# One fixed expert fewer in the expert stage, and the shared expert's hidden pieces in blocks 2, 3 and 4

## The chip, the cores and the metric

The kernel runs on one core of a Trainium2 chip, in one launch. The metric is device time in microseconds (us) from the start to the end of an execution. The engines are called as in the profile: PE (TensorE, with PEld for its weight loads), DVE (VectorE), ACT (ScalarE), POOL (GpSimd) and SP (SyncE, which here only issues DMAs).

## What is computed

The reference applies two transformer-like blocks to 512 tokens of width 1024, in float32. The first has a gated delta rule with a convolution beside it, and then a mixture of experts; the second has a state-space mixer and a dense feed-forward layer. The change touches the mixture of experts alone, which the reference writes so (cut):

```python
scores = jax.nn.sigmoid((hf @ router_w).astype(jnp.float32))
...
_, top_idx = lax.top_k(jnp.where(exp_keep, sel, -jnp.inf), TOP_K)
...
def expert_block(args):
    tok, e = args
    return swiglu(h_pad[tok], w_gate[e], w_up[e], w_down[e])
...
routed = jnp.zeros((t + 1, d), h.dtype).at[slot_tok].add(weighted)[:t]
return (routed + swiglu(hf, s_gate, s_up, s_down)).reshape(bsz, n, d)
```

Each of the 512 tokens goes to 6 of 64 experts. Each expert is a gated feed-forward net with hidden width 256: gate and up matrices of 1024 x 256, a down matrix of 256 x 1024, 3 MB together. Every token also passes through one shared expert of the same size.

## The kernel before

**Blocks and ranks.** How many tokens an expert gets is known only on the chip, but the program's shape is fixed. So the kernel counts the tokens of the experts, sorts them by that count and gives the expert of each rank a place with a fixed number of rows (`CAPS`, by rank: 256, 192, 152, 128, ... 16). `plan` (from L1071) makes 42 blocks of up to 128 rows of it. The first 18 ranks (`NPAIR`) have an expert alone in a block (the largest three in two blocks), ranks 18 to 43 share a block two by two ("pair", 64 rows each), ranks 44 to 59 four by four ("quad", 32 rows each). Tokens beyond a rank's rows go to overflow blocks in a loop at the end; with the given inputs there are none, before or after the change.

The last four experts (`NFIX`) are left out of the sorting. They have fixed blocks 0 to 3 of 128 rows, and their weights are known without a count. So these blocks can run while DVE, ACT and POOL still build the tables of the ranked ones (`places`, `table`). The order before is: blocks 0 to 3 fixed, 4 quad, 5 and 6 rank 0, 7 and 8 rank 1, 9 quad, 10 and 11 rank 2, 12 quad, 13 rank 3, 14 quad, 15 rank 4, 16 pair, 17 rank 5, 18 pair, and from there a pair after each single rank, to block 41.

**One block** (`blocks` L1643, `ffn` L1597). POOL gathers the block's token rows from DRAM (`X<-hrow,tok`, L1593; `tokf` in place of `tok` in a fixed block). PE transposes them (`pt_xb`, 8 instructions, the copies L1341 and L1343 on ACT and DVE apply a scale and a shift), multiplies by the gate and up weights (`gub`, 16 instructions of 512 columns, 32 in a pair, 64 in a quad), ACT and DVE form the gated hidden (`sgb` L1615, `hb` L1617), PE transposes it (`pt_hb`) and multiplies by the down weights (`pyb`). POOL adds the rows to the result in DRAM (`yacc<-yb,tok`, L1639). The time of a matmul is set by its 512 columns and not by how many of the block's rows are filled. In a pair or quad the experts' matmuls run beside each other on parts of the array.

**Weights.** An expert is three loads of 1 MB on SP's queue: parts 0 and 1 for `gub`, part 2 for `pyb` (L1525; a ranked expert's number is read by a register load at L1511 ahead of them). A quad's order is four parts 0, four parts 1, four parts 2. Loads go in turn to a ring of 10 slots (`ew0` to `ew9`), from `more()` behind the tables on to 12 (two more, `ewx`, where the tables' one-hot rows were). A load waits until PE has read what the slot held 12 loads earlier; SP issues loads in order and keeps eight outstanding. The shared expert's three parts lie in slots of their own from early on.

**The shared expert's pieces.** Its hidden is made in four pieces of 16 matmuls (`shared`, L1540): `sg` of the first half ahead of block 0, and `su`, `sg`, `su` behind the blocks that `HID` names, 10, 11 and 12. Its output is four pieces of 8 matmuls (`spy`, `shared_out`, L1557) behind the blocks of `OUT`, 13 to 16. The hook of block 17 (`SECOND`) gives its three slots to the ring in place of the two `ewx`, and starts loads and DVE work for the second transformer block; until the slots are free SP waits there. A hook's code is written behind its block's `ffn`, so its matmuls stand behind that block's `pyb`. They need no weights from the ring.

**The order** on each engine is the order in which the instructions are written, but for what a scheduler moves by a few places, such as the `pt_xb` of the next block ahead of `pyb`.

In `body`, blocks 0 and 1 are written, then `table`, `more()`, and then

```python
            moe.blocks(bp, ps, {HID[0]: hid(0, 1), HID[1]: hid(1, 0), HID[2]: hid(1, 1), OUT[0]: out(0), OUT[1]: out(1), OUT[2]: out(2), OUT[3]: out(3), SECOND: second}, (2, len(BLOCKS)))
```

Of the kernel before, what the change touches and what calls it, by code (L numbers as in the profile page):

```python
# [826 lines left out]
def block_one(k, pool, early, two, route):  # L827
# [7 lines left out]
    with ExitStack() as es:  # L835
# [215 lines left out]


NE = 64
NFIX = 4
NRK = NE - NFIX
NPAIR, NQUAD = 18, 44
CAPS = [256, 192, 152, 128, 124, 118, 108, 100, 92, 88, 86, 82, 79, 76, 75, 72, 70, 68, 64, 64, 62, 62, 59, 57, 56, 54, 54, 52, 51,
        50, 49, 46, 45, 44, 44, 43, 42, 41, 41, 40, 39, 38, 37, 37, 32, 32, 32, 31, 30, 30, 28, 26, 25, 23, 22, 20, 20, 18, 17, 16]
CAPS = [-(-c // 16) * 16 for c in CAPS]
NOV = 72  # L1060
# [4 lines left out]
RINGX = 3  # L1065


HID, OUT, SECOND = (10, 11, 12), (13, 14, 15, 16), 17


def plan():  # L1071

    fixed = [(e, P, [("fix", NRK + e)]) for e in range(NFIX)]
    one, more, b, r = [], [], NFIX, 0
    while r < NRK:
        n = 1 if r < NPAIR else 2 if r < NQUAD else 4
        c = CAPS[r]
        if n == 1:
# [6 lines left out]
        else:  # L1085
            more.append([(b, P, [("rank", r + i) for i in range(n)])])
            assert max(CAPS[r:r + n]) <= P // n
            b += 1
# [22 lines left out]
NSLOT = NB * P  # L1111
STEP = [-(-c // P) * P if r < NPAIR else 64 if r < NQUAD else 32 for r, c in enumerate(CAPS)] + [P] * NFIX
CST2 = ["iota", "low", "col", "base", "cap"]


def const2():
# [6 lines left out]

        "base": np.broadcast_to(np.resize(np.concatenate([NFIX * P + np.cumsum([0] + STEP[:NRK - 1]), np.arange(NFIX) * P]), P)[:, None], (P, P)),
        "cap": np.broadcast_to(np.resize(np.array(CAPS + [P] * NFIX), P)[:, None], (P, P)),
    }
# [23 lines left out]
class Moe:  # L1150
# [426 lines left out]
    def parts(self, n):  # L1577
# [7 lines left out]
        t = {0: self.tok, 32: self.tok2, 64: self.tok3, 96: self.tok4}  # L1585
        return [(a, t[a][0:CAPS[r], b:b + 1]) for a, (_, r) in zip(range(0, P, m), whos)]

# [922 lines left out]
```

## Time and profile before

| | |
|---|---|
| time before, median of 3 runs | 2020.23 us (2017.06 to 2023.76) |
| the profiled execution, its own time | 2015.22 us |
| its span in the profile, mean granted clock | 2013.3 us, 0.968 |
| PE busy in the span | 1826.9 us (91%) |
| DVE, ACT, POOL busy | 993.3, 596.5, 502.1 us |
| expert weights: 192 loads of 1 MB in three names | `ewrank` x168, `ewx` x12, `ewfix` x12 |
| the first `gub` of block 0 | 587.61 us |
| the first `gub` of the first quad (block 4) | 645.67 us |

The chain that ended last runs mostly through PE, and is shared by many lines; in the expert stage `gub`, `pyb` and the loads of `ewrank` are its largest parts. The stage's blocks run from 587.61 us to about 1210 us. In it, read PE's busy time together with the share of the DMA engines: a window with a DMA share of 1.0 has all 16 DMA engines busy with weights and rows, a share below that has engines that stand still for part of it. The profiled execution is 5 us below the median of the three runs, and within 2 us of the lowest.

### The profile page before, as it was taken

How to read it: one execution, taken by the hardware profiler on the slowest of the kernel's cores; microseconds unless marked ns; L12 is line 12 of the kernel's file. 1: busy time of each engine (PE TensorE's matmuls, PEld its weight loads, DVE VectorE, ACT ScalarE, POOL GpSimd, SP SyncE). 2: the span in 40 equal slices, each digit the busy share in tenths (PEclk: the TensorE clock that was granted, in tenths of full speed). 3: DMA queues.
4: the chain of work that ended last, by engine and by line, in shares of the span. 5: the costliest groups of instructions: out<-in, count | busy, mean ns of one | idle time of the engine just before them, and what ended most of it. 6: DMA issues, size and time to landing. Idle time of an engine off the chain costs nothing.

```text
span 2013.3 us, 24229 instructions
## 1 busy us (share of the span) xinstructions
PE 1826.9 (91%) x8481; PEld 1237.6 (61%) x8481; DVE 993.3 (49%) x2220; ACT 596.5 (30%) x1124; POOL 502.1 (25%) x407
## 2 busy tenths in 40 slices
PE   5897778996879999989999987999999999999998
PEld 3686556885644333333333335888888788888886
DVE  4689955668776222262222227776423453323352
ACT  5453311213423111111111114433423344323341
POOL 1314343442422222212212225342001113101300
PEclk9998988998989999999999998999999999999999
DMA  8354353226488998999999983332323423233241
GB/s 313 118 179 161 88 163 99 80 60 214 151 299 300 355 369 346 350 398 380 367 366 370 375 321 127 111 106 79 115 89 92 143 85 105 89 94 100 79 141 42
DMA packets 135555, 393.64 MB, mean 196 GB/s; under 512 B 46899, under 2 KB 59443, under 8 KB 109064
## 3 DMA queue, kind: packets, MB, share of 16 engines
q1 hardware_dynamic: 109752, 363.66, 50.7%
q0 software_dynamic: 11856, 26.83, 5.3%
q10 hardware_dynamic: 13824, 1.58, 0.5%
q8 instruction: 68, 1.11, 0.2%
q14 instruction: 55, 0.45, 0.1%
HBM read 365.19 MB, written 38.54 MB: 201 GB/s over the span
## 4 chain that ended last, share of the span: by engine, by line
PE 69%; DVE 15%; DMA 10%; ACT 3%; issue 2%; POOL 1%; SPq 0%; another core or an unknown queue 0%; ACTq 0%; POOLq 0%; DVEq 0%
PE psi L139 12%; PE gub L139 10%; PE pof L139 9%; PE psf L139 9%; PE pyb L139 6%; DMA ewrank<-ew 6%; PE psco L139 2%; DVE cfa L746 2%; PE poo L139 2%; DVE gt L569 1%; PE pxca L139 1%; PE pt_xb L142 1%; PE pm L139 1%; PE psga L139 1%; PE psgb L139 1%
## 5 line engine op out<-in xcount | busy, mean ns | idle before, releaser
L139 PE MATMUL gub<-ewrank,xTb 128*64 128x512 f32 (+5 forms) x960 | 266.6, 596 | 1.2 <-DMA ewrank<-ew 0.6
L274 DVE TENSOR_TENSOR wlo<-wraw,whi 128x1024 fp32r<-128x1024 f32 (+1 forms) x103 | 121.7, 1182 | 137.7 <-ACT whi L273 136.9
L139 PEld LDWEIGHTS gub<-ewrank,xTb 128*64 128x64 f32 (+5 forms) x960 | 90.0, 141 | 158.3 <-issue 144.1
L273 ACT CAST whi<-wraw 128x1024 fp32r<-128x1024 f32 (+1 forms) x115 | 113.8, 989 | 226.5 <-PE psi L139 50.6
L139 PE MATMUL pyb<-ewrank,hTb 128*64 128x512 f32 (+5 forms) x440 | 152.4, 607 | 3.4 <-DMA ewrank<-ew 1.4
L139 PE MATMUL psi<-xnh,whi 128*128 128x512 f32 (+1 forms) x368 | 141.2, 385 | 0.0
L139 PE MATMUL psi<-xnl,whi 128*128 128x512 f32 (+1 forms) x368 | 140.9, 383 | 0.0
L1617 DVE SCALAR_TENSOR_TENSOR hb<-gub,tw,sgb 128x256 f32<-128x256 f32 (+5 forms) x38 | 18.3, 482 | 230.3 <-ACT sgb L1615 230.3
L1639 POOL DMA_INDIRECT yacc<-yb,tok x61 | 86.1, 1411 | 158.3 <-DVE yb L1631 109.3
L1341 ACT ACTIVATE xTb<-pt_xb,B,A 128x128 f32<-128x128 f32 (+5 forms) x168 | 74.0, 445 | 173.2 <-DVE xTb L1343 171.8
L139 PE MATMUL psi<-xnh,wlo 128*128 128x512 f32 (+1 forms) x296 | 112.8, 381 | 0.0
L1593 POOL DMA_INDIRECT X<-hrow,tok x38 | 39.6, 1042 | 291.2 <-PE pt_xb L142 285.9
L1343 DVE TENSOR_SCALAR xTb<-pt_xb,A,B 128x128 f32<-128x128 f32 (+5 forms) x168 | 65.5, 392 | 88.2 <-PE pt_xb L142 51.9
L2433 POOL TENSOR_TENSOR fr<-fr 128x512 f32<-128x512 f32 x32 | 48.6, 1518 | 238.2 <-ACT fr L2432 238.2
L139 PE MATMUL psf<-xml,whi 128*128 128x512 f32 (+1 forms) x272 | 102.6, 377 | 0.2 <-DVE xml L274 0.2
L139 PE MATMUL psf<-xmh,whi 128*128 128x512 f32 (+1 forms) x272 | 102.5, 378 | 0.2 <-ACT xmh L273 0.2
L139 PE MATMUL psf<-xmh,wlo 128*128 128x512 f32 (+1 forms) x272 | 102.5, 377 | 0.0
L1631 DVE TENSOR_TENSOR yb<-pyb,gt 128x512 f32<-128x512 f32 (+5 forms) x84 | 57.9, 690 | 72.0 <-PE pyb L139 70.5
L1615 ACT ACTIVATE sgb<-gub 128x256 f32<-128x256 f32 (+5 forms) x42 | 16.0, 382 | 260.3 <-PE gub L139 260.3
L139 PEld LDWEIGHTS pyb<-ewrank,hTb 128*64 128x64 f32 (+5 forms) x440 | 46.4, 142 | 74.9 <-issue 63.7
L139 PEld LDWEIGHTS psi<-xnh,whi 128*128 128x128 f32 x368 | 69.2, 189 | 13.8 <-issue 0.2
L139 PEld LDWEIGHTS psi<-xnl,whi 128*128 128x128 f32 x368 | 69.2, 188 | 13.4
(755 smaller groups left out, 4030.1 us busy)
## 6 DMA issues: line engine op xcount, KB each, us to landing
ewrank<-ew SPq DMA_DIRECT2D x168, 1024.0 KB, 25.1
wraw<-w_in SPq DMA_DIRECT2D x59, 512.0 KB, 3.7
wraw<-ff SPq DMA_DIRECT2D x32, 512.0 KB, 3.5
wf<-ff SPq DMA_DIRECT2D x64, 256.0 KB, 2.7
wm<-w_mod SPq DMA_DIRECT2D x28, 512.0 KB, 7.8
ewfix<-ew SPq DMA_DIRECT2D x12, 1024.0 KB, 16.9
ewx<-ew SPq DMA_DIRECT2D x12, 1024.0 KB, 19.6
wm<-w_mod SPq DMA_DIRECT2D x10, 1024.0 KB, 6.2
```

Source lines behind the costliest of these rows:

```text
L139: return self._done(self.eng.matmul(out, lhsT, rhs, **kw), rate, rhs)
L142: return self._done(self.eng.transpose(out, in_, ident), 0.00118, ident)
L273: nc.scalar.copy(hi, raw)
L274: (eng or nc.vector).tensor_tensor(lo, raw, hi.bitcast(F32), ALU.subtract)
L569: eng.tensor_tensor(t, S[0:nq, w:32, b:w].to_broadcast([nq, n, b]), S[0:nq, b:w, 0:b].to_broadcast([nq, n, b]), ALU.mult)
L746: V.scalar_tensor_tensor(a[:, r0 * 64:r1 * 64], y[:, (r0 + o) * 64:(r1 + o) * 64], w[:, j, 15 + o:16 + o], a[:, r0 * 64:r1 * 64], ALU.mult ...
L1341: nc.scalar.activation(dst(c), pt[:, i, :], AF.Identity, scale=sa, bias=sb)
L1343: nc.vector.tensor_scalar(dst(c), pt[:, i, :], sa, sb, ALU.mult, ALU.add)
L1593: self.k.nc.gpsimd.indirect_dma_start(out=X[0:idx.shape[0]], out_offset=None, in_=self.hrow, in_offset=bass.IndirectOffsetOnAxis(ap=idx, a ...
L1631: nc.vector.tensor_tensor(y[0:n, cs], py[0:n], self.gt2[0:n, cs], ALU.mult)
L1639: self.k.nc.gpsimd.indirect_dma_start(out=self.yacc[1 - self.nsc % 2], out_offset=bass.IndirectOffsetOnAxis(ap=idx, axis=0), in_=y[a:a + n ...
L2433: nc.gpsimd.tensor_tensor(r, r, r, ALU.mult)
```

## The change

`NFIX` goes from 4 to 3. Experts 61 to 63 keep fixed blocks, now 0 to 2. The expert that was the first fixed one joins the sorted ones, which are now 61 ranks: 19 alone, 26 in pairs, 16 in quads (`NPAIR, NQUAD = 19, 45`), with one more rank of 68 (80 after rounding up to 16) rows in `CAPS`. There are 42 blocks as before; one fixed block of 128 rows less, and one block of 80 rows more, near the end. All blocks in between move forward by one number: 0 to 2 fixed, 3 quad, 4 and 5 rank 0, 6 and 7 rank 1, 8 quad, 9 and 10 rank 2, 11 quad, 12 rank 3, 13 quad, 14 rank 4, 15 pair, 16 rank 5, 17 pair. `HID` goes from (10, 11, 12) to (2, 3, 4). `OUT` and `SECOND` keep their block numbers, and so lie one block later in the sequence.

```diff
-NFIX = 4
+NFIX = 3
 NRK = NE - NFIX
-NPAIR, NQUAD = 18, 44
-CAPS = [256, 192, 152, 128, 124, 118, 108, 100, 92, 88, 86, 82, 79, 76, 75, 72, 70, 68, 64, 64, 62, 62, 59, 57, 56, 54, 54, 52, 51,
+NPAIR, NQUAD = 19, 45
+CAPS = [256, 192, 152, 128, 124, 118, 108, 100, 92, 88, 86, 82, 79, 76, 75, 72, 70, 68, 68, 64, 64, 62, 62, 59, 57, 56, 54, 54, 52, 51,
...
-HID, OUT, SECOND = (10, 11, 12), (13, 14, 15, 16), 17
+HID, OUT, SECOND = (2, 3, 4), (13, 14, 15, 16), 17
```

The first place is PE's instructions behind `gub` of block 2. Before, from `pt_hb` of block 2 to `gub` of block 3, which is fixed (`ewfix`):

```order
L142 MATMUL pt_hb_5022<-cst,hb_5020 128x128 x2
L142 MATMUL pt_xb_5049<-cst,X_4567 128x128 x4
L139 MATMUL pyb_5028<-ewfix_2_4592,hTb_5025 128x512 x2
L139 MATMUL pyb_5032<-ewfix_2_4592,hTb_5025 128x512 x2
L142 MATMUL pt_xb_5058<-cst,X_4567 128x128 x4
L139 MATMUL gub_5067<-ewfix_0_5039,xTb_5048 128x512 x4
L139 MATMUL gub_5067<-ewfix_1_5041,xTb_5048 128x512 x4
```

After, from the same `pt_hb` to the start of `gub` of block 3, now the quad (`ewrank`), on PE:

```order
L142 MATMUL pt_hb_5017<-cst,hb_5015 128x128 x2
L139 MATMUL pyb_5023<-ewfix_2_4592,hTb_5020 128x512 x2
L139 MATMUL pyb_5027<-ewfix_2_4592,hTb_5020 128x512 x2
L139 MATMUL su_5031<-h_3610,ewshared_0_3915 128x512 x4
L139 MATMUL su_5031<-h_3610,ewshared_1_3917 128x512 x4
L142 MATMUL pt_xb_5111<-cst,X_4567 128x128 x4
L142 MATMUL pt_xb_5120<-cst,X_4567 128x128 x4
L139 MATMUL gub_5129<-ewrank_0_5085,xTb_5110 32x512
```

The piece `su` now stands between the last fixed block and the first quad, and all eight transposes of the quad's rows stand behind it, where four of them stood ahead of `pyb`.

The second place is PE's instructions in the two blocks of rank 2 and up to the quad behind them. Before, from `pyb` of rank 2's first block:

```order
L139 MATMUL pyb_5704<-ewx_4986,hTb_5701 128x512 x2
L139 MATMUL pyb_5708<-ewx_4986,hTb_5701 128x512 x2
L139 MATMUL su_5712<-h_3610,ewshared_0_3915 128x512 x4
L139 MATMUL su_5712<-h_3610,ewshared_1_3917 128x512 x4
L139 MATMUL gub_5757<-ewrank_0_5659,xTb_5738 32x512 x4
L139 MATMUL gub_5757<-ewx_4986,xTb_5738 32x512 x4
L142 MATMUL pt_hb_5770<-cst,hb_5768 128x32 x2
L142 MATMUL pt_xb_5864<-cst,X_4567 128x128 x3
L139 MATMUL pyb_5776<-ewx_4986,hTb_5773 32x512 x2
L139 MATMUL pyb_5780<-ewx_4986,hTb_5773 32x512 x2
L139 MATMUL sg_5784<-h_3610,ewshared_0_3915 128x512 x4
L139 MATMUL sg_5784<-h_3610,ewshared_1_3917 128x512 x4
```

After, the same two blocks on PE, from the same `pyb` to the start of the quad's `gub`:

```order
L139 MATMUL pyb_5676<-ewrank_2_5633,hTb_5673 128x512 x2
L139 MATMUL pyb_5680<-ewrank_2_5633,hTb_5673 128x512 x2
L139 MATMUL gub_5718<-ewrank_0_5629,xTb_5699 32x512 x4
L139 MATMUL gub_5718<-ewrank_1_5631,xTb_5699 32x512 x4
L142 MATMUL pt_hb_5731<-cst,hb_5729 128x32 x2
L142 MATMUL pt_xb_5814<-cst,X_4569 128x128 x3
L139 MATMUL pyb_5737<-ewrank_2_5633,hTb_5734 32x512 x2
L139 MATMUL pyb_5741<-ewrank_2_5633,hTb_5734 32x512 x2
L142 MATMUL pt_xb_5814<-cst,X_4569 128x128
L142 MATMUL pt_xb_5823<-cst,X_4569 128x128 x4
L139 MATMUL gub_5832<-ewrank_0_5788,xTb_5813 32x512
```

The two pieces between the blocks are gone, and so is the third behind the quad: from quad to quad PE now has only the work of the blocks.

## Rows read from the trace of the kernel before

**Rows 1.** the profile's page: shares of the chain by engine and line

```profile
PE psi L139 12%; PE gub L139 10%; PE pof L139 9%; PE psf L139 9%; PE pyb L139 6%; DMA ewrank<-ew 6%; PE psco L139 2%; DVE cfa L746 2%; PE poo L139 2%; DVE gt L569 1%; PE pxca L139 1%; PE pt_xb L142 1%; PE pm L139 1%; PE psga L139 1%; PE psgb L139 1%
```

**Rows 2.** windows: us; busy PE, PEld, DVE, ACT, POOL (instructions); clock; DMA share; GB/s

```profile
635.00:695.00 60.00, 53.26 (x229) 23.07 (x228) 23.81 (x112) 11.76 (x30) 14.52 (x12) 1.00 1.02 385
695.00:715.00 20.00, 19.02 (x82) 6.44 (x84) 5.41 (x11) 3.52 (x10) 4.77 (x4) 1.00 0.85 270
715.00:755.00 40.00, 36.79 (x151) 13.79 (x144) 8.08 (x17) 5.21 (x14) 9.06 (x7) 1.00 1.01 383
755.00:770.00 15.00, 14.93 (x84) 5.65 (x86) 2.46 (x6) 2.26 (x5) 2.38 (x2) 1.00 0.57 207
770.00:840.00 70.00, 65.37 (x280) 26.07 (x273) 18.50 (x35) 10.34 (x24) 17.94 (x14) 1.00 1.02 403
840.00:855.00 15.00, 13.86 (x60) 5.65 (x57) 4.13 (x8) 1.67 (x4) 2.80 (x3) 1.00 0.69 234
```

**Rows 3.** the chain in order of time: start us, us, what

```profile
672.53 6.88 PE gub L139 x16
...
685.48 6.88 PE gub L139 x16
...
711.13 7.12 PE gub L139 x64
...
720.25 3.64 PE pyb L139 x32
...
737.02 6.87 PE su L139 x16
...
756.17 7.06 PE sg L139 x16
...
796.70 3.43 PE spy L139 x8
...
809.69 1.92 PE pyb L139 x8
...
817.71 3.55 PE pyb L139 x20
821.26 7.08 PE gub L139 x16
```

**Rows 4.** the stage's start, in timelines of DVE, PE and POOL

```profile
572.96 2.50 DVE L1494 TENSOR_TENSOR onehots<-iota,fx_pl 128x512 fp32r<-128x512 f32 x4
...
631.59 7.03 PE L139 MATMUL gub<-ewfix,xTb 128*128 128x512 f32 x16
...
645.67 4.06 PE L139 MATMUL gub<-ewrank,xTb 128*32 128x512 f32 x35
...
625.63 1.11 POOL L1593 DMA_INDIRECT X<-hrow,tok  x1 [4.39 <-DVE tok L1464]
```

**Rows 5.** waits of SP's queue, 640 to 720 us (total, times, longest)

```profile
SPq L1525 <- PE gub L139: 33.2, 10, 16.0
```

**Rows 6.** DMA queues, 715 to 815 us: packets, MB, share of the 16 engines

```profile
q1 hardware_dynamic: 4528, 33.01, 80.4%
q0 software_dynamic: 1641, 3.62, 14.0%
```

**Rows 7.** windows of two late periods, columns as in group 2

```profile
951.60:979.50 27.90, 25.75 (x92) 9.54 (x92) 6.77 (x14) 5.00 (x12) 6.27 (x5) 1.00 1.00 367
1064.30:1093.50 29.20, 26.69 (x93) 9.30 (x93) 6.71 (x14) 4.92 (x12) 6.35 (x5) 1.00 1.01 375
```

**Rows 8.** waits of PE, 560 to 1260 us (total, times, longest)

```profile
PE pyb L139 <- DMA ewrank<-ew: 1.4, 3, 0.9
```

**Rows 9.** a window behind a long wait of PE, and the chain around it

```profile
880.00:900.00 20.00, 17.87 (x56) 7.86 (x57) 11.12 (x32) 3.79 (x9) 4.06 (x3) 0.88 1.02 407
...
846.88 3.70 PE pyb L139 x16
...
882.71 4.66 PE pyb L139 x16
```

## The prediction

> **What bounds the kernel now.** I read the page first: its table of engines has PE busy for 91% of the span, and the chain by line has `gub` and `pyb` of the experts beside one DMA, the expert weights [rows 1]. So PE's work counts nearly everywhere, and weights can count in the expert stage. There the windows decide [rows 2]. From 635 to 695, 715 to 755 and 770 to 840 us the DMA share is 1.01 or 1.02: the stream of weights and rows has no room. It stands still in part at three places: 695 to 715 (0.85 of 20 us, 3.0 us idle), 755 to 770 (0.57 of 15, 6.5 us) and 840 to 855 (0.69 of 15, 4.6 us). The chain shows what PE does at the second of these: one of the shared expert's pieces, `sg`, right behind another, `su` [rows 3]. Such a piece takes PE's time and frees no slot of the ring. Yet PE hardly waits for weights: `pyb` for `ewrank` 1.4 us in the whole stage [rows 8]. So the stage is balanced: the stream is full, PE is full, and the shared expert's pieces give the stream its time just where the three quads (blocks 9, 12, 14) want 12 loads each. The question is what happens when that cover is taken away.
>
> **The start.** One fixed expert fewer takes one of the four one-hot operations ahead of the first gather off DVE, 2.50 us for four [rows 4], so 0.6 us. The first ranked block's rows are asked for at 625.63 us [rows 4]. In the changed kernel PE wants them when `pyb` of block 2 and the piece `su` are done. `gub` of block 3 begins at 631.59 before, and the 6.87 us of `su` [rows 3] come in its place, so at 631.0 + 6.9 = 637.9 us. That leaves the gather 12 us. I cost it at nothing; `su` is the cover, and without it PE would wait for the rest of the gather. Start: **-0.6 us**.
>
> **The exchanged block.** From `gub` of block 3 to `gub` of the first quad are 645.67 - 631.59 = 14.1 us, which go [rows 4]. A single block has a period of 685.48 - 672.53 = 12.95 us [rows 3], which comes back near the end. Fewer rows don't shorten it: its matmuls keep their 512 columns. **-1.1 us**.
>
> **The moved pieces.** PE's work in them stays: three pieces of some 7.0 us (6.87 and 7.06 in [rows 3]), 21.0 together. What changes is what the weights do meanwhile.
>
> At blocks 2 to 4 the pieces hold PE for 21.0 us while the ring can't run ahead. A load needs the slot that PE has read, and SP's queue stood for 33.2 us behind `gub` in 640 to 720 us already [rows 5]; by 695 to 715 the stream idles for want of slots. The change puts more PE time there (21.0 less the 14.1 of the block that left) and takes three loads away. So the time is lost to the stream, and the ring is just as full, twelve loads, when the quad now numbered 8 comes. Its `gub` starts at 711.13 - 0.6 - 14.1 + 21.0 = 717.4 us.
>
> From there to `pyb` of the third quad (block 13 now) I hold PE's need against the stream's.
> - PE: before, 809.69 - 711.13 = 98.6 us [rows 3]. Without the three pieces and the output piece `spy` of 3.4 us, which lies behind block 13 afterwards, 74.1 us. Without a wait `pyb` would begin at 791.5.
> - Stream: 30 loads of 1.049 MB (12 + 3 + 12 + 3 of the next quad, rank and quad start from slots that the first quad frees). In 715 to 815 us the queue of SP carried 33.01 MB in 80.4 us of all engines' time, and the rows of tokens took 14.0 us [rows 6]. So 31.5 MB take 76.6 us, with the rows 90.6. The first slots come free with the half of a quad's `gub` (7.12 us), 3.6 us in: 721.0. The last weights land about 811.6.
>
> So PE waits 811.6 - 791.5 = **+20.1 us**, first in the quad that is block 11, then in block 13. Before, this stretch had a loss of its own: from 809.69 to 821.26 PE spent 11.6 us on `pyb` of the third quad and a `spy`, cut into pieces, where 3.64 and 3.43 are their durations elsewhere [rows 3]. With a few tenths between them that is some 4.1 us, which the new wait contains: **-4.1 us**.
>
> **Late in the stage.** A period of one single block and one pair takes 27.9 us early (951.60 to 979.50) and 29.2 late (1064.30 to 1093.50), with the DMA share at 1.00 and 1.01 [rows 7]. Five such late periods lose 6.5 us to the stream. Afterwards PE arrives later there: -0.6 - 1.1 + 20.1 - 4.1 = +14.3 us. The stream ends its third quad about when it did, and then has three loads more (7.7 us) and one block's rows (14.0 us for the six blocks 9 to 14, so some 2.3 us): at most +10. So it has more lead than before, and part of the 6.5 us comes back; the bounds are 0 and 6.5. I take **-4 us**, over half, since even the early period has a share of 1.00.
>
> **The clock.** Behind PE's long wait of before (6.5 us for `hb`) the granted clock was 0.88 over 20 us, so in part at the lower of the two levels, 1.2 GHz, and `pyb` of a pair took 4.66 instead of 3.70 us [rows 9]. Two long waits would cost 1 us each: **+2 us**, between 0 and 4. The Trainium skill (TensorE: Matmul & The Clock Gate, Part 1) says that an idle PE falls back to 1.2 GHz; the trace agrees with its 0.88.
>
> **Sum.** -0.6 - 1.1 + 20.1 - 4.1 - 4 + 2 = +12.3 us. On the profiled execution of 2015.2 us that gives 2027.5. This execution is near the fastest of the runs; their median is 2020.2, and on it the sum gives **2032.5 us**.
>
> **Rivals.**
>
> *Faster: the stream runs ahead.* If the ring is not full while the pieces run at blocks 2 to 4, the engines use these 21 us, quads 11 and 13 find their weights, and the wait of 20.1 us is gone with both losses of before: -0.6 - 1.1 - 4.1 - 6.5 = -12.3, 2007.9 us. It decides by the DMA's idle time between 640 and 718 us: each microsecond less takes one off the wait, and below 6 us of wait the kernel is faster by more than 0.3%. For it speaks that the share is 1.02 up to 695, so the ring is not full all the time. Against it: the twelve slots can't hold any load of block 11's quad but those behind the first quad's reads, whatever the lead [rows 5]. Chance 0.08.
>
> *No change to speak of: the stream is quicker in one long burst.* At the 403 GB/s of 770 to 840 us [rows 2] the 30 loads and their 3.4 MB of rows take 34.9 / 0.403 = 86.6 us, and the wait is 16 us. With all 6.5 us of the late loss regained and no loss by the clock: -0.6 - 1.1 + 16 - 4.1 - 6.5 = +3.7, 2024 us. Chance 0.20.
>
> *Heavier: nothing comes back.* At the 367 GB/s of the early period [rows 7] the same 34.9 MB take 95.1 us, the wait is 24.6 us, the late loss stays and the clock costs 2: +20.8, 2041 us. Chance 0.14. The Trainium skill (DMA: Bandwidth & Descriptors, Specifications) gives about 358 GB/s as HBM's limit for a core; by that the 34.9 MB would take an estimated 97.5 us and the wait would be 27 us. The trace has 403 GB/s over 70 us, so I don't hold to it.
>
> *It doesn't do what it says.* The order of PE's instructions has the pieces behind blocks 2, 3 and 4 and none between the later quads, so I give this nothing.
>
> **Chances and range.** A difference below 0.3% (6 us) can't be told from no change here. The forecast itself, from the +8 to +16 us that the bounds of its late and clock terms allow, has 0.58. Slower by over 0.3% are the forecast and the heavier case, 0.72. Within 0.3%: the second rival, 0.20. Faster: 0.08. The range reaches from below the second rival's 2024 to just above the heavier case's 2041, 2018 to 2042; what lies outside is the faster case (0.08) and the tails of the two others, some 0.1 together.
>
> **What would show it.** Right: the DMA share from 640 to 718 us well below the 1.02 of before, and near 1.0 from 720 to 811 without the gap at 755 to 770; PE's waits for `ewrank` at `gub` or `pyb` of blocks 11 and 13 near 20 us, where the stage had 2; late periods of 28 us and not 29.2; the granted clock below 1.00 around 770 to 810. Wrong: if PE waits for `X` of the first quad, the start was not covered; if `gub` of block 8 starts near 717 but no wait for weights follows, the ring held more than I think, and the first rival was right; if the late periods stay at 29.2, or grow, the stream and not PE ends the stage, and the time is that of the heavier case. The place is tested by `gub` of block 14: by the sum it starts near 811.6 + 3.6 + 3.4 = 819 us, against 821.26 before [rows 3], with one `spy` and one single block more to come.

## The result

The changed kernel takes 2031.2 us (median of 6 runs, 2028.69 to 2033.06) against 2019.38 us before (6 runs, 2017.06 to 2023.76): a ratio of 1.006, 95% interval 1.0048 to 1.0071. It is 12 us slower. The sum of the prediction had said +12.3 us, 2032.5 us, inside 2018 to 2042.

The profiled execution of the changed kernel took 2032.45 us, that of before 2015.22. So the two traces differ by 17.2 us where the medians differ by 11.8: before's execution is 4 us faster than its median, the other 1 us slower. Sizes of effects are therefore taken from medians here, and places and the lengths of single steps from traces.

The windows of the changed kernel at the borders of [rows 2], and from 680 to 851 us at borders that fit its own blocks (columns as there):

```profile
635.00:695.00 60.00, 54.79 (x225) 23.70 (x225) 21.11 (x96) 10.45 (x25) 12.64 (x10) 1.00 0.88 319
695.00:715.00 20.00, 18.02 (x54) 6.94 (x53) 4.39 (x10) 3.63 (x10) 2.52 (x2) 1.00 0.62 151
...
755.00:770.00 15.00, 13.34 (x89) 4.81 (x88) 3.38 (x8) 3.28 (x8) 2.41 (x2) 1.00 1.02 406
...
680.00:720.00 40.00, 36.95 (x127) 14.93 (x130) 10.15 (x22) 7.67 (x19) 7.31 (x7) 1.00 0.66 189
772.00:812.00 40.00, 29.51 (x119) 9.11 (x119) 5.86 (x12) 3.88 (x9) 8.98 (x7) 0.91 1.02 404
812.00:828.00 16.00, 15.57 (x52) 4.72 (x53) 4.31 (x8) 2.20 (x5) 1.05 (x1) 1.00 0.96 392
```

The DMA share is the eighth figure. It was 1.02 from 635 to 695 and 0.85 to 715; now it is 0.88 and 0.62, and from 680 to 720 only 0.66, with PE busy for 36.95 of 40 us. The gap at 755 to 770 is closed (0.57 before, 1.02 now). Behind it, at 772 to 812, the share is 1.02 and PE is busy for 29.51 of 40 us (37.52 before): where the kernel before had idle DMA time, this one has idle PE time, a hundred microseconds later.

SP's queue in 640 to 720 us shows why the stream stood still, as in [rows 5], where it was 33.2 us in all and 16.0 the longest:

```profile
SPq L1525 <- PE gub L139: 57.2, 6, 24.9
```

The loads wait for slots that PE has still to read, and the pieces behind blocks 2, 3 and 4 don't read any.

The second and the third quad (blocks 11 and 13) in PE's timeline (start us, us, line, operation, count, and in brackets the idle time before and what ended it):

```profile
766.38 2.56 PE L139 MATMUL pyb<-ewrank,hTb 128*32 128x512 f32 x8
...
769.56 1.90 PE L139 MATMUL pyb<-ewrank,hTb 128*32 128x512 f32 x4
...
772.03 3.62 PE L139 MATMUL pyb<-ewrank,hTb 128*32 128x512 f32 x20 [0.31 <-DMA ewrank<-ew]
775.58 3.70 PE L139 MATMUL gub<-ewrank,xTb 128*128 128x512 f32 x8
...
788.73 1.72 PE L139 MATMUL gub<-ewrank,xTb 128*32 128x512 f32 x6
792.50 4.41 PE L139 MATMUL gub<-ewrank,xTb 128*32 128x512 f32 x28 [2.04 <-DMA ewrank<-ew]
800.27 1.04 PE L139 MATMUL gub<-ewrank,xTb 128*32 128x512 f32 x2 [3.36 <-DMA ewrank<-ew]
803.67 1.91 PE L139 MATMUL gub<-ewrank,xTb 128*32 128x512 f32 x2 [2.35 <-DMA ewrank<-ew]
806.16 4.76 PE L139 MATMUL gub<-ewrank,xTb 128*32 128x512 f32 x26 [0.58 <-DMA ewrank<-ew]
811.98 0.44 PE L142 MATMUL pt_hb<-cst,hb 128*128 128x128 f32 x2 [1.05 <-DVE hb L1617]
```

From the first `gub` of the third quad to its `pt_hb` are 23.3 us. In the kernel before, the same step of its third quad took 8.2:

```profile
800.50 4.06 PE L139 MATMUL gub<-ewrank,xTb 128*32 128x512 f32 x35
...
808.74 0.44 PE L142 MATMUL pt_hb<-cst,hb 128*128 128x128 f32 x2 [1.16 <-DVE hb L1617]
```

Of the 15 us between them, PE's rows name 8.3 us of waits for `ewrank`; the rest stands in matmuls that the record shows as long (13.8 us of busy time for 64 that take 7.1 elsewhere). The list of waits, 788 to 812 us, has most of that rest in the row of the weight loads, PEld:

```profile
PEld gub L139 <- DMA ewrank<-ew: 13.3, 5, 4.3
```

Whoever goes by PE's row alone finds little more than half. Some 1.2 us more are the clock's: from 804 to 808 us the granted clock is 0.50, the lower level, and behind the last wait PEld goes from one group of four loads to the next in 0.86 us until 808.6, and in 0.43 from then on (busy time and the idle time ahead of it):

```profile
804.00:808.00 4.00, 3.42 (x14) 0.53 (x16) 0.00 (x0) 0.00 (x0) 0.00 (x0) 0.50 1.01 426
...
807.01 0.20 PEld L139 LDWEIGHTS gub<-ewrank,xTb 128*32 128x32 f32 x4 [0.66 <-issue]
...
809.04 0.12 PEld L139 LDWEIGHTS gub<-ewrank,xTb 128*32 128x32 f32 x4 [0.31 <-issue]
```

Behind it come the third quad's `pyb`, with the first output piece among them:

```profile
812.93 1.90 PE L139 MATMUL pyb<-ewrank,hTb 128*32 128x512 f32 x4
814.76 1.13 PE L139 MATMUL spy<-ewshared,shh 128*128 128x512 f32 x2
815.82 1.90 PE L139 MATMUL pyb<-ewrank,hTb 128*32 128x512 f32 x4
...
819.56 1.13 PE L139 MATMUL spy<-ewshared,shh 128*128 128x512 f32 x2 [0.35 <-DVE h L1568]
820.62 1.90 PE L139 MATMUL pyb<-ewx,hTb 128*32 128x512 f32 x4
...
827.06 7.13 PE L139 MATMUL gub<-ewrank,xTb 128*128 128x512 f32 x16
```

The next `gub` starts at 827.06, 14.1 us after the first `pyb`; 3.64 and 3.43 would be due [rows 3]. Before, the same step, also with one output piece in it, took 11.5 us (809.69 to 821.19 in PE's timeline, 821.26 in the chain of [rows 3]). No weight is waited for in these rows. The four `pyb` of one expert are written in a row and use the same quarter of the array, so they take 1.90 us by themselves, where 32 of four experts side by side take 3.64.

Late in the stage, two periods of one single block and one pair:

```profile
1042.70:1070.50 27.80, 25.61 (x93) 9.18 (x93) 6.71 (x14) 4.92 (x12) 6.30 (x5) 1.00 1.00 374
1070.50:1098.20 27.70, 25.55 (x92) 9.10 (x92) 6.71 (x14) 4.92 (x12) 6.35 (x5) 1.00 1.01 375
```

They last 27.7 to 27.8 us, as the early period of before (27.9) and not as its late one (29.2) [rows 7].

### The profile page after: what moved, and what is told of

Read it like the earlier page. It is cut to its first block, busy times and chain, and to the rows that moved or that the text cites. A ratio compares the mean times of both kernels' runs of the same rounds, so it can differ in the third digit from the quotient of the medians.

```text
span 2030.6 us, 24226 instructions
## 1 busy us (share of the span) xinstructions
PE 1834.3 (90%) x8477; PEld 1235.5 (61%) x8477; DVE 993.4 (49%) x2219; ACT 595.7 (29%) x1124; POOL 502.3 (25%) x407
## 4 chain that ended last, share of the span: by engine, by line
PE 71%; DVE 16%; DMA 6%; ACT 3%; issue 2%; POOL 1%; SPq 0%; another core or an unknown queue 0%; ACTq 0%; POOLq 0%; DVEq 0%
PE gub L139 12%; PE psi L139 12%; PE pof L139 9%; PE psf L139 9%; PE pyb L139 8%; PE psco L139 2%; DVE cfa L746 2%; PE poo L139 2%; DMA ewrank<-ew 1%; DVE gt L569 1%; PE pt_xb L142 1%; PE pxca L139 1%; PE pm L139 1%; PE psga L139 1%; DVE soq L462 1%
## 5 line engine op out<-in xcount | busy, mean ns | idle before, releaser
L139 PE MATMUL gub<-ewrank,xTb 128*64 128x512 f32 (+5 forms) x976 | 276.6, 601 | 10.7 <-DMA ewrank<-ew 8.3
L139 PE MATMUL pyb<-ewrank,hTb 128*64 128x512 f32 (+5 forms) x464 | 163.8, 607 | 2.8 <-ACT hTb L1622 0.8
L139 PEld LDWEIGHTS psi<-xnh,whi 128*128 128x128 f32 x368 | 69.6, 190 | 13.9 <-issue 0.2
```

What stands on the lines that cost most here:

```text
L139: return self._done(self.eng.matmul(out, lhsT, rhs, **kw), rate, rhs)
```

## The experiments

Theory A: the pieces' place is what costs, through the weight stream, which stands still for want of slots while they run. Rival B: the exchanged expert costs. Theory C, formed on the trace above: part of the loss is the order inside the third quad. All runs are compared with the kernel before on the same chip; ratios have 95% intervals.

**The two parts of the change, apart.** The first run keeps three fixed experts and puts the pieces back where they stood in the sequence:

```diff
-HID, OUT, SECOND = (2, 3, 4), (13, 14, 15, 16), 17
+HID, OUT, SECOND = (9, 10, 11), (13, 14, 15, 16), 17
```

> The changed kernel with the three hidden pieces back at the places of the sequence where they were before (blocks 9, 10 and 11 in the new count); three fixed experts stay. Theory A (the pieces' new place starves the weight stream: it idles at 680 to 720 us for want of slots, and PE then waits in the third quad): the idle stretch and the wait are gone, DMA share of 680 to 720 us back to 0.9 or more, under 3 us of waits for ewrank at gub and pyb, and the time falls by 10 to 14 us to 2017 to 2022 us. Rival B (it is the exchanged expert that costs, a late single block for a fixed one): the time stays at 2028 to 2033 us.

Measured: 2016.43 us (11 runs), ratio 0.9986 (0.9977 to 0.9995), 3 us below the kernel before and 15 below the changed one. The second has four fixed experts and moves the pieces alone:

```diff
-HID, OUT, SECOND = (10, 11, 12), (13, 14, 15, 16), 17
+HID, OUT, SECOND = (3, 4, 5), (13, 14, 15, 16), 17
```

> The kernel before with its four fixed experts, and only the pieces moved, to blocks 3, 4 and 5, which are the last fixed block, the first quad and the first block of rank 0, as in the changed kernel. Theory A (the pieces' place alone): 2030 to 2036 us, with the DMA share at 0.6 to 0.8 around 690 to 725 us and some 8 us of waits for ewrank at gub of block 14, the third quad. Rival B (the exchanged expert): no change, 2016 to 2023 us.

Measured: 2038.73 us (5 runs), ratio 1.0097 (1.0082 to 1.0112), 20 us slower, more than expected. Windows of the first run, then of the second, from 680 us on:

```profile
680.00:720.00 40.00, 36.79 (x178) 13.77 (x177) 9.91 (x21) 7.21 (x18) 8.78 (x7) 1.00 0.91 314
772.00:812.00 40.00, 37.42 (x160) 14.05 (x159) 9.63 (x19) 6.08 (x14) 7.58 (x7) 1.00 1.02 404
```

```profile
680.00:720.00 40.00, 36.85 (x107) 16.97 (x106) 9.25 (x20) 7.19 (x18) 7.45 (x7) 1.00 0.77 253
812.00:851.00 39.00, 30.93 (x107) 8.71 (x100) 4.80 (x9) 2.59 (x6) 3.73 (x3) 0.87 0.98 391
```

With the pieces back the stream's idle share is gone and PE is busy for 37.42 of 40 us at the third quad, which waits for no weight. With the pieces moved both signs are there, and the third quad, later in this kernel, has PE busy for 30.93 of 39 us. So the pieces' place costs, as A had it, and B falls: the run with the exchanged expert alone (with its output pieces one block later in the sequence) is 3 us faster, and the pieces cost 15 (three fixed) to 20 us (four). Whether the loss comes about as A says is left to the runs with short pieces.

**Why 15 and not 20.** With the pieces back, the first quad of the changed order has no `su` ahead of it. The row of its `pt_hb` in that run:

```profile
642.49 0.51 PE L142 MATMUL pt_hb<-cst,hb 128*128 128x128 f32 x2 [2.48 <-DVE hb L1617]
```

PE waits 2.48 us for `hb` where 1.1 is usual, and the granted clock is 0.59 from 642 to 646 us: the whole step from `pt_hb` of block 2 to that of block 4 is 30.9 us there (626.82 to 657.76), and in the changed kernel 42.4 (624.39 to 666.74) with 13.9 us of pieces in it, so 28.4 without. The piece behind block 2 hides some 2.5 us. With four fixed experts nothing is hidden: the step is 26.7 us before (640.70 to 667.44), and with the pieces 41.7 (642.80 to 684.53), so 27.8 without them.

Another part is the order inside the third quad. From its first `pyb` to the next `gub` the run with the pieces back takes 14.1 us, as the changed kernel does. The run with the pieces alone takes 14.1 as well, where the kernel before, with its output pieces behind the same blocks, took 11.5:

```profile
796.57 1.90 PE L139 MATMUL pyb<-ewrank,hTb 128*32 128x512 f32 x4
...
810.70 7.13 PE L139 MATMUL gub<-ewrank,xTb 128*128 128x512 f32 x16
```

```profile
831.58 1.90 PE L139 MATMUL pyb<-ewx,hTb 128*32 128x512 f32 x4
...
845.71 7.13 PE L139 MATMUL gub<-ewrank,xTb 128*128 128x512 f32 x16
```

So with four fixed experts the move of the pieces also changes how the third quad is written, which costs 2.6 us, and with three it does not. The whole sum, stretch by stretch, is in the table further down.

**What a piece costs where it stands.** Both kernels with the three pieces cut to an eighth:

```diff
-        for i in range(8):
+        m = 1 if up or f else 8
+        for i in range(m):
...
-                             start=(i == 0), stop=(i == 7))
+                             start=(i == 0), stop=(i == m - 1))
```

> The changed kernel with each of the three moved pieces cut to one of its eight matmul steps, behind blocks 2, 3 and 4; seven eighths of the shared hidden are left out, some 18.4 us of PE work. Theory A (there the pieces hold up the weight stream): the idle share of 680 to 720 us and the wait in the third quad shrink, and the time falls by 10 to 16 us, to 2015 to 2021 us, and comes within 4 us of the next run. Rival E (PE's work alone sets the time, wherever it stands): this run and the next each fall by 18 us, to 2013 and 1998 us.

Measured: 2018.17 us (10 runs), ratio 1.000 (0.9987 to 1.0013), 13 us less than the changed kernel.

> As the run with the pieces back at blocks 9, 10 and 11 (2016.4 us), with the same three pieces cut to one of eight steps there. Theory A (at 9 to 11 the stream of weights needs that time anyway, and PE would wait for weights in place of it): the time falls by 5 us at most, 2011 to 2017 us, and 10 us or more of waits for weights appear in the second and third quad. Rival E: it falls by the 18 us that are left out, to 1998 us.

Measured: 2015.4 us (10 runs), ratio 0.9988 (0.9978 to 0.9997), 1.0 us less than with the whole pieces by the medians, and nothing by the ratios (0.9986 there). So 18.4 us of PE work were worth 13 us behind blocks 2 to 4 and 1 us at most behind 9 to 11. Rival E, by which PE's work counts wherever it stands, falls. In the latter run 7.5 us of waits for `ewrank` are named at `gub` in PE's row and 13.8 in PEld's, where there were none with the whole pieces.

One expectation of theory A failed. With the pieces cut short at 2 to 4 the stream stands still less (share 0.86 at 680 to 720 us, not 0.66), but the wait in the third quad does not shrink: 8.1 us are named, 8.3 in the changed kernel:

```profile
680.00:720.00 40.00, 36.78 (x177) 13.65 (x176) 10.09 (x22) 7.68 (x19) 8.43 (x7) 1.00 0.86 288
...
PE gub L139 <- DMA ewrank<-ew: 8.1, 4, 3.4
```

The rows of `pt_hb` show what happens. The changed kernel, its blocks 0, 8 (the first ring-bound quad) and 13 (the third), the last one above at 811.98:

```profile
595.10 0.44 PE L142 MATMUL pt_hb<-cst,hb 128*128 128x128 f32 x2 [1.80 <-DVE hb L1617]
...
725.47 0.44 PE L142 MATMUL pt_hb<-cst,hb 128*128 128x128 f32 x2 [1.16 <-DVE hb L1617]
```

The run with the whole pieces behind 9 to 11:

```profile
597.53 0.44 PE L142 MATMUL pt_hb<-cst,hb 128*128 128x128 f32 x2 [0.99 <-DVE hb L1617]
...
709.61 0.44 PE L142 MATMUL pt_hb<-cst,hb 128*128 128x128 f32 x2 [1.16 <-DVE hb L1617]
...
795.62 0.44 PE L142 MATMUL pt_hb<-cst,hb 128*128 128x128 f32 x2 [1.08 <-DVE hb L1617]
```

With an eighth of them there, blocks 8 and 13:

```profile
709.01 0.44 PE L142 MATMUL pt_hb<-cst,hb 128*128 128x128 f32 x2 [1.16 <-DVE hb L1618]
...
795.98 0.44 PE L142 MATMUL pt_hb<-cst,hb 128*128 128x128 f32 x2 [1.05 <-DVE hb L1618]
```

With an eighth of them behind 2 to 4, blocks 0, 8 and 13:

```profile
598.12 0.44 PE L142 MATMUL pt_hb<-cst,hb 128*128 128x128 f32 x2 [2.00 <-DVE hb L1618]
...
712.45 0.44 PE L142 MATMUL pt_hb<-cst,hb 128*128 128x128 f32 x2 [1.16 <-DVE hb L1618]
...
798.34 0.44 PE L142 MATMUL pt_hb<-cst,hb 128*128 128x128 f32 x2 [1.05 <-DVE hb L1618]
```

Six kernels by such rows, in us; with four fixed experts the blocks are 9, 14 and 15 in place of 8, 13 and 14:

| kernel | `pt_hb` of block 0 to 8 | 8 to 13 | 13 to 14 | 14 to the last block |
|---|---|---|---|---|
| before (four fixed) | 121.9 | 89.5 | 20.6 | 377.1 |
| pieces alone (four fixed) | 143.7 | 87.4 | 23.2 | 378.3 |
| pieces back (three fixed) | 112.1 | 86.0 | 23.2 | 387.0 |
| changed (three fixed) | 130.4 | 86.5 | 23.2 | 386.9 |
| short pieces at 2 to 4 | 114.3 | 85.9 | 23.2 | 386.2 |
| short pieces at 9 to 11 | 112.5 | 87.0 | 23.2 | 386.8 |

With three fixed experts the move adds 18.3 us ahead of block 8 (21 less the 2.5 that are hidden), and the stretch from 8 to 13 doesn't get shorter by the 21 us of pieces that left it: 18.3 + 0.5 + 0 - 0.1 us in the four columns. With four fixed experts they are 21.8 - 2.1 + 2.6 + 1.2, 5 us more. In this stretch there are two limits of nearly the same length, as its windows in the two runs with pieces at 9 to 11 show, whole and short:

```profile
709.61:795.62 86.01, 80.51 (x363) 31.77 (x363) 18.06 (x37) 12.65 (x31) 20.34 (x16) 1.00 0.94 370
```

```profile
709.01:795.98 86.97, 74.00 (x321) 24.94 (x321) 18.07 (x37) 12.65 (x31) 20.37 (x16) 0.94 1.02 403
```

With the whole pieces the stream has room (0.94) and PE waits for no weight: the 86.0 us are PE's own, 65.0 of blocks (before: 89.5 less 24.4 of pieces) and 21.0 of pieces. With short ones, or none, PE waits for weights and the share is 1.02. So the stream's standing still at 680 to 720 us is not what makes the wait. The wait is there with and without work in front; what the move does is to put 21 us of PE's work where nearly all of it counts, and to take it out of a stretch that the weights make as long without it.

**The order inside the third quad.** The changed kernel with its output pieces one block later:

```diff
-HID, OUT, SECOND = (2, 3, 4), (13, 14, 15, 16), 17
+HID, OUT, SECOND = (2, 3, 4), (14, 15, 16, 17), 18
```

> The changed kernel with the output pieces one block later (behind 14 to 17, the second block's preparation behind 18), so that no spy stands inside the third quad's pyb. Theory C (the 14.2 us from the first pyb of the third quad to the next gub come from the order on PE: its pyb are written expert by expert between pieces of spy, so that they don't run beside each other; 7 us are lost to it, not to weights): the stretch without spy takes some 6 us, and the time falls by 4 to 7 us to 2024 to 2027 us. Rival D (PE is there as late as the weights let it be, and the order is hidden behind the stream): the time stays within 2 us of 2031.

Measured: 2025.17 us (5 runs), ratio 1.0034 (1.002 to 1.0047), 6 us less than the changed kernel, as C had it. From the first `pyb` of its third quad to the next `gub` are 8.0 us (811.04 to 819.03). But two numbers moved. The preparation of the second transformer block alone, behind 18:

```diff
-HID, OUT, SECOND = (2, 3, 4), (13, 14, 15, 16), 17
+HID, OUT, SECOND = (2, 3, 4), (13, 14, 15, 16), 18
```

> The changed kernel with the preparation of the second transformer block behind block 18 in place of 17, and nothing else. Theory F (of the 6 us that the run with the outputs moved had gained, about half came from this: SP's wait there falls from 21.9 us, and DVE's work of it lies elsewhere): 2025 to 2029 us, with SP's wait at that place under 15 us. Rival C (all of it came from the third quad's pyb being written without pieces of spy between): within 2 us of 2031.

Measured: 2033.21 us (5 runs), ratio 1.008 (1.0067 to 1.0094): no gain, though SP's wait there fell from 21.9 to 14.6 us as F wanted, so F falls. And the first output piece alone, out of the third quad, one block earlier:

```diff
-HID, OUT, SECOND = (2, 3, 4), (13, 14, 15, 16), 17
+HID, OUT, SECOND = (2, 3, 4), (12, 14, 15, 16), 17
```

> The changed kernel with its first output piece behind block 12, ahead of the third quad, in place of behind 13, the others behind 14 to 16, and the second block's preparation behind 17 as it was. The third quad's pyb has no spy inside, as in the run with the outputs moved, but that run's other edit (preparation behind 18) is not in it. Theory C (the order inside the third quad): the piece stands where PE waits for weights anyway, so it is free (3.4 us), and the quad's pyb take 3 us less: 2024 to 2027 us. Rival G (the run with the outputs moved gained by having the last output piece in the stretch of the preparation, not by the quad): 2029 to 2033 us.

Measured: 2028.56 us (6 runs, 2025.92 to 2032.61), ratio 1.0053 (1.0034 to 1.0071), between what C and its rival expected. Its third quad:

```profile
811.92 1.90 PE L139 MATMUL pyb<-ewrank,hTb 128*32 128x512 f32 x4
...
814.01 1.90 PE L139 MATMUL pyb<-ewrank,hTb 128*32 128x512 f32 x4
...
819.91 7.13 PE L139 MATMUL gub<-ewrank,xTb 128*128 128x512 f32 x16
```

Eight microseconds from the first `pyb` to the next `gub` in place of 14.1, of which 3.4 are the piece that left; two experts are still written by themselves. In this one trace `pt_hb` of block 14 comes at 828.04 and not 835.19, 6.6 us less counted from `pt_hb` of block 0 (594.51 and 595.10); the medians show 2.6 us, and the intervals of the two ratios overlap. By the rows 3.4 of the 6.1 us are the piece, which PE now does where it would wait for weights, and 2.7 are the order. So that the order costs time is shown by the rows; its price in the whole time isn't. The run with the outputs moved has the same 2.7 us. Its other 3.4 are the piece, too: from block 14 to the last block it takes 386.3 us with one output piece more than the changed kernel has there in 386.9. So its gain comes about half from the order, as C has it, and half from a piece that costs nothing where it stands now, which is nearer to rival G.

**Together.**

```diff
-HID, OUT, SECOND = (2, 3, 4), (13, 14, 15, 16), 17
+HID, OUT, SECOND = (9, 10, 11), (14, 15, 16, 17), 18
```

> Pieces back at blocks 9, 10 and 11 and output pieces behind 14 to 17, with three fixed experts. If theories A and C both hold, the gains add up to some 16 to 20 us: 2012 to 2016 us, faster than the kernel before. If C falls, it is as the run with the pieces back, 2017 to 2022 us; if A falls, 2024 to 2031 us.

Measured: 2016.48 us (12 runs), ratio 0.998 (0.9968 to 0.9992): the gains don't add up. The third quad's later `pyb` in this run:

```profile
804.82 1.90 PE L139 MATMUL pyb<-ewx,hTb 128*32 128x512 f32 x4 [0.99 <-DMA ewx<-ew]
807.31 0.62 PE L139 MATMUL pyb<-ewx,hTb 128*32 128x512 f32 x1 [0.59 <-DMA ewx<-ew]
```

With PE on time, part 2 of the quad's weights is only just landing: from the first `pyb` to the next `gub` are 11.5 us (799.35 to 810.86), where the run with the outputs moved has 8.0, so what the order no longer takes the stream does. In the changed kernel PE is so late there that no weight is waited for, and the order counts. C and D are both right, each in its kernel.

**One piece early.** From the first pair of runs, one piece behind block 2 hides 2.5 us, and the stream of the run with the pieces back still idles for some of 680 to 772 us:

```diff
-HID, OUT, SECOND = (2, 3, 4), (13, 14, 15, 16), 17
+HID, OUT, SECOND = (2, 9, 11), (14, 15, 16, 17), 18
```

> Three fixed experts, the first piece behind block 2 and the others behind 9 and 11, outputs behind 14 to 17 and the preparation behind 18. Theory A with a lead to spare: the run with all pieces back leaves the stream some 9 us idle between 680 and 772 us, so one piece of 7 us may go, and behind block 2 it covers the rows that the first quad waits for (2 to 3 us): 2010 to 2015 us, the fastest of all. Rival: any piece that leaves the stretch between the quads costs its 7 us there: 2018 to 2024 us.

Measured: 2014.25 us (11 runs), ratio 0.998 (0.9968 to 0.9991), 4.4 us less than before by the medians: the lowest of all, though its ratio is that of the run with both edits. One more piece between the quads:

```diff
-HID, OUT, SECOND = (2, 9, 11), (14, 15, 16, 17), 18
+HID, OUT, SECOND = (2, 9, 11), (12, 14, 15, 16), 18
```

> The fastest kernel so far (first piece behind block 2, others behind 9 and 11) with the first output piece behind block 12 and the others behind 14 to 16, preparation behind 18. Theory A (what stands between the quads is free up to some 21 us, and 14 stand there): another 3.4 us are free, 2009 to 2013 us. Rival: the stretch is full with two pieces; no change from 2014.3 us, within 2 us.

Measured: 2015.15 us (12 runs), ratio 0.9988 (0.9977 to 1.000): nothing gained. Its trace has 82.9 us from `pt_hb` of block 8 to that of 13 (714.61 to 797.46), against 81.7 in the run ahead of it (712.62 to 794.33): part of the 3.4 us is hidden there, and no more comes of it. The stretch with one piece early:

```profile
712.62:794.33 81.71, 74.53 (x346) 28.27 (x347) 17.17 (x36) 12.59 (x31) 20.33 (x16) 1.00 1.00 390
```

So the weights can let PE through in 81.7 us, and 86 is not fixed: 31.9 MB moved in it (81.71 us at 390 GB/s), against 35.0 in the run with short pieces behind 9 to 11. Why it is some three loads less isn't shown.

## Why the prediction was right, point by point

- **The start** (-0.6): the one-hots take 1.90 us for three where it was 2.50 for four, as computed. Block 0 starts 1.6 us earlier in this trace; but in the traces with three fixed experts its `pt_hb` lies anywhere from 593.4 to 598.3 us, so a term of this size can't be read from one. The first quad's rows were covered by `su`; its `gub` starts at 638.66, 0.8 us later than worked out, since it waits 1.93 us for `xTb`: all eight transposes now stand behind `su`. That wait wasn't foreseen.
- **The exchanged block** (-1.1): with the start, -1.7 us forecast. The run with the pieces back is 2.6 us faster than before (0.9986, -1 to -4.6 within its interval), but that sum also holds the late term below, the order of the third quad (+2.6) and its uncovered first quad, so the term is not measured by itself.
- **The first ring-bound quad**: `gub` forecast at 717.4, found at 717.31.
- **The wait** (+20.1): first `pyb` of the third quad forecast at 811.6, found at 812.93, so 21.4. Of it 15 us stand in the third quad's `gub`, 1.2 of them the clock's, and 5.6 in the second quad's `pyb` (9.2 us from 766.38 to 775.58, for 3.64). These `pyb` are also written in part expert by expert, with 0.3 us of wait named, so weights and order aren't told apart in that smaller part. The mechanism is shown by the short pieces: the stretch takes 86 to 87 us with PE's pieces in it or without, and with or without pieces in front of it, as it must if the ring is just as full when the first ring-bound quad comes. The stream ran at 404 GB/s over 40 us there. The Trainium skill (DMA: Bandwidth & Descriptors, Specifications) has about 358 GB/s as HBM's limit for a core; the measurement decides, and the longer wait by that figure did not come.
- **Before's own loss** (-4.1): this step failed. It was taken for a wait for weights that the new wait would contain. It was the order of `pyb` and `spy`, fixed when the program is built, and the step grew from 11.5 to 14.1 us. The term should have been +2.6: the two kernels' orders stood open to view, and I had not held the third quad's `pyb` of the one against the other. The prediction's own test of the place missed by it: `gub` of block 14 was to start near 819, and starts at 827.06.
- **Late** (-4, bounds 0 and 6.5): the periods are 27.8 us, so all of it came back, some 6.5. But the reason failed: the periods were to shorten since PE arrives later. In the run with the pieces back PE is at the third quad 16 us earlier than in the changed kernel (795.62 and 811.98), and the time from block 14 to the end is the same, 387.0 and 386.9 us. In the run with the pieces alone PE is 22 us later than before (830.62 and 808.74), and nothing comes back, 378.3 against 377.1. One block (12.95) and one `spy` (3.43) more would make 393.5 of the 377.1, so 6.6 us came back, and they come with the exchanged expert, not with the late PE. What in the exchange gives them is open. Other than the section on the change has it, the blocks move forward by one number only up to 24: the additional single block is not near the end but number 25, so that two single ones stand in a row (`pt_hb` at 989.15 and 1001.78) ahead of the late periods, and from 26 on the numbers are those of before. A single block needs three loads where a pair needs six, so the stream may gain its lead there; no run tests it. That the term had the right sign and over half of its size is luck.
- **The clock** (+2): the granted clock is 0.91 in 772 to 812 us, so in part at the lower level, and 1.00 again from 812 to 828. Most of the low time is spent waiting for weights; behind the last wait the rows show 1.2 us, which the 21.4 of the wait contain. So one long wait cost what was forecast for it, 1 us, and for a second one there is no row (the granted clock is 1.00 from 770 to 788 us, at the second quad's wait).

With these the terms are -0.6 - 1.1 + 21.4 + 2.6 - 6.6 = +15.7 us. By the traces `pt_hb` of the last block comes 15.7 us later (1222.08 and 1206.39), the whole executions are 17.2 apart, and the medians 12. So the right sum owes something to errors that cancel in part (+6.7 on the order, -2.6 late, -2 on the clock, +1.3 on the wait), to a late term that is right for another reason, and to medians that lie closer together than the two profiled executions; the direction, the place and the size of the wait were right. The first rival (the stream runs ahead) fell by the DMA share of 0.66 at 680 to 720 us, the second and third by the wait of 21 us.

## What to carry to other kernels

Work that needs nothing from a transfer stream belongs where the stream is the limit, and there it can be free: 18 us of matmuls were worth 1 us at one place and 13 us at another. Where a ring is full, such work put in front costs nearly its whole time: the stream can't use it to run ahead, and the wait that the work used to cover stands open behind it, at the largest group of loads. Before a stretch is charged to a wait, look at the order of its instructions: a loss that stands between rows without any wait named is one of order.

## What was not expected of the hardware

A quad's matmuls on four quarters of the array run beside each other only while neighbouring instructions use different quarters: 32 `pyb` take 3.64 us, and four of one expert by themselves 1.90 us, some four times their share of 0.46. And PE's row in the list of waits named 8.3 us where one quad was 15 us longer than before: records of matmuls at a stall are long themselves (six of a quad's 64 took 1.72 us, at a granted clock of 1.00). The row of PEld named 13.3.
